# The causal mask added by VectorE instead of by an identity product, with new waits, in a hybrid decoder layer

## The chip, the cores and the metric

The program runs on one core of a Trainium2 chip. A core has five engines with queues of their own, each strictly in order: TensorE (PE; its weight loads are shown apart as PEld), VectorE (DVE), ScalarE (ACT), GpSimd (POOL) and SyncE (SP), which here only starts transfers. PE writes its results into PSUM, eight banks of 128 x 512 float32 numbers; DVE and ACT read and write both PSUM and the large on-chip memory, SBUF. The metric is the time of one execution on the device in microseconds (us).

## What is computed

One decoder layer on 256 tokens of width 1024: a combined projection whose columns are split into block-sparse attention (MoBA, 8 heads of 64) and retention (4 heads), an output projection, cross attention, and a gated feed-forward net, each with its norms and its residual. With 256 tokens there is a single key block, so that the attention is plain causal attention:

```python
proj = h @ w_in[l]
mq, mk, mv, rq, rk, rv, rg = jnp.split(proj, SPLIT_POINTS, axis=-1)
...
s_own = jnp.einsum('bhqd,bhld->bhql', qb, k_own).astype(jnp.float32) * scale
own_pos = cur * L + key_offsets
s_own = jnp.where(own_pos[None, :] <= q_pos[:, None], s_own, NEG_INF)
...
p = jax.nn.softmax(logits, axis=-1)
...
mix = jnp.concatenate([mo, ro], axis=-1) @ w_out[l]
x = x + rms_norm(mix, g_post_mix[l])
```

The change concerns the line with `jnp.where`: the scores of keys that lie after the query are made so small that their exponential is zero.

## The kernel before

Tokens lie in two tiles of 128 (t = 0 and 1). Weights come in blocks of 128 x 1024 float32 numbers, one transfer each, into a ring of six raw buffers (`rawp`, line 76); the block number q is in the names `raw13` and `hl13`. Each block is **split** (`split_weight`, lines 196 and 197): ACT copies it into a rounded form, DVE subtracts that from the original, and both parts together are `hl<q>`, in a ring of nine. A product with a block takes three passes of PE, high by high, high by low and low by high (lines 1114 to 1116), each 128 x 512.

The program is a list of **steps**, one for each piece of weight product, and PE executes them in that order. The side work (evictions, rotations, softmax, norms) is written as generators: each does a piece, yields a number from the table `WAIT` (line 38), and goes on that many steps later (`run_side`, line 259). So `WAIT` decides behind which weight product a piece stands, on every engine, and in which order the pieces stand on ACT and DVE. A weight block is split at the end of a step in which no side work ran, or when it is nearly due (line 1185 on). [...]

The first stage is the input projection in six chunks of columns: chunk 0 gives the queries, 1 the keys, 2 the retention's queries and keys (`ret_qk`), 3 its values, 4 its gate, 5 the attention's values. Each chunk has an accumulator for each token tile, named `acc<step>`: acc17 and acc18 are chunk 2, acc25 and acc26 chunk 3, acc33 and acc34 chunk 4. From chunk 2 on they come from a pool of **three** banks (`psB`, line 84). Chunk 3's are evicted by ACT into `rvd` (line 241). Transposes (c_q, c_k, c_r, c_R_mem, c_ro) all use **one** bank (`psC`, line 85), which ACT evicts. Softmax uses four banks (`psS`, line 83).

The attention is done in three units: m00 (queries of tile 0, all eight heads, 128 keys), m10 and m11 (queries of tile 1, four heads each, 256 keys). A unit goes in this order (`softmax_unit`, line 291; `moba_unit`, line 334): PE computes the scores into two banks `s_m`, and adds the mask there with a product of an identity matrix and the mask (lines 345 and 356: ahead of the scores in m11, behind them in the others); DVE takes the maxima (302) and their negative `nb` (306); ACT the exponentials (312); DVE normalizes (315, 317); PE transposes (`pt_m`, 325). Inside m11, right after its scores, the retention's scores `rs` are started.

Other names: `x_load` (line 1027) loads x and the constants on SP's queue; `x_stats` (1033) casts identity and mask for the products and has ACT take the mean squares of x (`junk`, 224); `mem_stats` (1011) does so for the memory rows. `xt_mix` and `xt_cross` (515) are the transposes of x behind the output projection and the cross attention; `xn` (509) is x scaled for the latter.

Of the kernel before, what the change touches and what calls it, by code (L numbers as in the profile page):

```python
# [8 lines left out]
F32R = mybir.dt.float32r  # L9
BF16 = mybir.dt.bfloat16  # L10
AF = mybir.ActivationFunctionType
ALU = mybir.AluOpType
AX = mybir.AxisListType

P = 128
# [21 lines left out]

WAIT = {
    "cpb0": 2, "cpb1": 1, "cpv0": 7, "cpv1": 1, "cu0": 3, "cu1": 4, "ex_c0": 2, "ex_c1": 1, "ex_m00": 0,
    "ex_m10": 0, "ex_m11": 4, "f0_0": 8, "f0_1": 5, "g_add": 1, "g_silu": 5, "gate0": 3, "gate1": 6,  # L40
    "gp1": 5, "gp2": 0, "k_add": 0, "k_hl": 3, "lag": 2, "ret": 9, "low": 6, "mq": 0, "mrow": 4, "ms": 21, "mst": 5,
# [5 lines left out]
}  # L47
WARM = 9

# [2 lines left out]
C_ID, C_MASK, C_MCOS, C_MSIN, C_RCOS, C_RSIN, C_DEC, C_END = 0, 128, 256, 288, 320, 448, 576, 1600  # L52
# [3 lines left out]
def tile_hybrid_layer(  # L56
# [14 lines left out]
    nc = tc.nc  # L71
    ctx.enter_context(tc.manual_schedule())

    cpool = ctx.enter_context(tc.tile_pool(name="cpool", bufs=1))
# [12 lines left out]
    def tok(t):  # L87
        return slice(t * P, (t + 1) * P)
# [4 lines left out]
    def small(name):  # L93
        return sm.tile([P, 8], F32, tag="sm", name=name)
# [10 lines left out]
    cst = cpool.tile([P, C_DEC], F32, tag="cst", name="cst")  # L105
    xg = cpool.tile([P, 288], F32, tag="xg", name="xg")
    gp = xg[:, 0:32].rearrange("p (g k) -> p g k", g=4)
    x_sb = cpool.tile([P, 2, D], F32, tag="x", name="x_sb")
    identb = cpool.tile([P, P], BF16, tag="identb", name="identb")
    maskb = cpool.tile([P, P], BF16, tag="maskb", name="maskb")  # L110
    identr = cpool.tile([P, P], F32R, tag="identr", name="identr")
    maskr = cpool.tile([P, P], F32R, tag="maskr", name="maskr")
    junk = cpool.tile([P, D], BF16, tag="junk", name="junk")
    mhalf = cpool.tile([P, 8], F32, tag="mhalf", name="mhalf")
    ident = cst[:, C_ID:C_ID + P]
# [5 lines left out]
    T = {}  # L121
# [3 lines left out]
    def need(*keys):  # L125

        missing = [k for k in keys if k not in emitted]
        assert not missing, missing
# [83 lines left out]
    def inv_rms(key, ss0, ss1=None, n=1):  # L212
        v = small(f"v_{key}")
        if ss1 is None:
            nc.vector.tensor_scalar(v[:, :n], ss0, EPS, None, op0=ALU.add)
        else:
            nc.vector.tensor_scalar(v[:, :n], ss0, ss1, EPS, op0=ALU.add, op1=ALU.add)
        r = cpool.tile([P, 8], F32, tag=f"r_{key}", name=f"r_{key}")
        nc.gpsimd.tensor_tensor(out=r[:, :n], in0=v[:, :n], in1=mhalf[:, :n], op=ALU.pow)
        rstd[key] = r  # L220
        return r

    def mean_square(dst, src, n):
        nc.scalar.activation(junk[:, :n], src, AF.Square, scale=1.0 / 32.0, accum_out=dst)
# [31 lines left out]
    def spawn(gen, wait=0):  # L256
        active.append([step_no[0] + wait, gen])
# [76 lines left out]
    def moba_unit(t, g):  # L334
        keys = P * (t + 1)
        n = D // keys
        hn = n // 2

        def fill(s):

            need(f"q{t}", *[f"k{u}" for u in range(t + 1)])

            ahead = g == 1
            for e in range(2) if ahead else ():
                nc.tensor.matmul(s[e].rearrange("p (h k) -> p h k", h=hn)[:, :, keys - P:keys], identr,
                                 maskr[:, None, :].to_broadcast([P, hn, P]), start=True, stop=False,
                                 skip_group_check=True)
            for i in range(hn):
                j = g * hn + i
                for e in range(2):  # L350
                    rows = slice(64 * e, 64 * e + 64)
                    nc.tensor.matmul(s[e][:, i * keys:(i + 1) * keys], T["qT"][rows, j, tok(t)],
                                     T["kT"][rows, j, 0:keys], start=(i == 0 and not ahead),
                                     stop=(ahead and i == hn - 1), skip_group_check=True)
            for e in range(2) if not ahead else ():
                nc.tensor.matmul(s[e].rearrange("p (h k) -> p h k", h=hn)[:, :, keys - P:keys], identb,
                                 maskb[:, None, :].to_broadcast([P, hn, P]), start=False, stop=True,
                                 skip_group_check=True)
            if ahead:
                scores = ret_scores()  # L360
                spawn(scores, next(scores))
            yield 0

        return softmax_unit(f"m{t}{g}", n, keys, 0.125, fill)

    def moba_units():
# [47 lines left out]
    def ret_scores():  # L414

        need("rqk0", "rqk1")
        for kb in range(2):
            n = P * (2 - kb)
            s = [accS(f"rs{kb}{e}") for e in range(2)]
            for j in range(2):  # L420
                for e in range(2):
                    rows = slice(64 * e, 64 * e + 64)
                    nc.tensor.matmul(s[e][:, j * n:(j + 1) * n], T["rkT"][rows, j, tok(kb)],
                                     T["rqT"][rows, j, kb * P:256], start=True, stop=True)
            for e in range(2):
                if kb == 0 or e == 0:
                    buf = tmp2k(f"ra{kb}{e}")
                a = buf[:, kb * e * 256:kb * e * 256 + 2 * n].rearrange("p (j i) -> p j i", j=2)
                T[f"ra{kb}{e}"] = a
                nc.vector.tensor_tensor(out=a, in0=s[e][:, 0:2 * n].rearrange("p (j i) -> p j i", j=2),  # L430
                                        in1=T["decay"].rearrange("p (j e) i -> p e j i", e=2)[:, e, :, 0:n], op=ALU.mult)
            if kb == 0:
                yield WAIT["rs"]
# [478 lines left out]
    for what in USE:  # L912
# [4 lines left out]
        elif what[0] == "d":  # L917
            k = int(what[1:])
# [17 lines left out]
    for q, item in enumerate(items):  # L936
        if item[0] == "w":
            continue
        kind, w, g, home, part, plus = item[:6]
# [91 lines left out]
        yield 0  # L1031

    def x_stats():
        nc.vector.tensor_copy(identb, ident)
        nc.vector.tensor_copy(maskb, cst[:, C_MASK:C_MASK + P])
        nc.vector.tensor_copy(identr, ident)
        nc.vector.tensor_copy(maskr, cst[:, C_MASK:C_MASK + P])
        for t in range(2):
            ss = small(f"ss_x{t}")
            mean_square(ss[:, 0:1], x_sb[:, t, :], D)  # L1040
            inv_rms(f"x{t}", ss[:, 0:1])
        yield 0
# [25 lines left out]
    x_split(2, 3)  # L1068
    opening = {4: lambda: x_split(4, 5), 7: lambda: x_split(6, 7)}
    late = {WAIT["xd"]: x_load, WAIT["xs"]: x_stats, WAIT["ms"]: mem_stats}  # L1070
    pending_split = list(range(2, NQ))

    accs, downs = {}, {}
    for i, s in enumerate(steps):
# [17 lines left out]
        if s[0] == "first":  # L1092
# [3 lines left out]
            h = hls[q][:, :, c * 512:(c + 1) * 512]  # L1096
# [6 lines left out]
        elif s[0] == "col":  # L1103
# [4 lines left out]
            h = hls[q].rearrange("p s (k n) -> p s k n", k=2)  # L1108
            for kk in range(2):
                k = 2 * kp + kk  # L1110
# [9 lines left out]
        elif s[0] == "row":  # L1120
# [13 lines left out]
            for k, w in ops:  # L1134
                begin = half == 0 and (k, w) == ops[0]
                end = half == 1 and (k, w) == ops[-1]
                if w:
                    nc.tensor.matmul(acc, hls[q][:, 0, k * P:(k + 1) * P], T[f"{st}_k"][:, k, :], start=begin, stop=end,  # L1138
                                     skip_group_check=True)
                else:  # L1140
                    nc.tensor.matmul(acc[:, 0:256], hls[q][:, 1, k * P:(k + 1) * P], T[st][:, 0, k, :], start=begin,  # L1141
                                     stop=end, skip_group_check=True)
            if half == 1:
                spawn(done(nt, acc))
        elif s[0] == "down":
            _, q, t, j, kk, halves = s
# [17 lines left out]
        elif s[0] == "seven":  # L1164
            _, q, g, m, part, name, begin = s
# [3 lines left out]
            h = hls[q].rearrange("p s (k n) -> p s k n", k=2)  # L1169
            for kk in range(2):  # L1170
                xh, xl = token_operand(m, 2 * part + kk)
                end = part == 1 and kk == 1
                for n, (a, w) in enumerate(((xh, 0), (xh, 1), (xl, 0))):
                    nc.tensor.matmul(acc, a, h[:, w, kk, :], start=begin and kk == 0 and n == 0, stop=end and n == 2,  # L1174
                                     skip_group_check=True)
# [9 lines left out]
        if pending_split:  # L1185
# [3 lines left out]
            hold = 0 <= i - starts["ffn"] + WAIT["hold0"] < WAIT["hold"] and q - s[1] > WAIT["hold_low"]  # L1189
            if q >= FFN_Q + 8:  # L1190
                paced = q not in after or split_at[after[q]] + WAIT["sum"] <= i
                near = due[q] - i <= (WAIT["near"] if i - split_at[q - 1] >= 2 else WAIT["now"])
            else:
                near = q - s[1] <= WAIT["low"]
# [113 lines left out]
```

## Time and profile before

| what | value |
|---|---|
| time, median of 3 runs | 398.38 us (398.0 to 398.8) |
| the profiled execution: its time | 400.7 us |
| its span, first to last instruction | 398.9 us |
| mean granted TensorE clock | 0.998 |
| DMA | 80.36 MB, mean 201 GB/s |

The granted clock of PE is at 90% or more in each of 40 slices of the span. DVE and ACT by slice (40 equal slices of 10 us, busy share in tenths):

```profile
DVE  3876877586869987677576699999899899999964
ACT  4885973964757865494547766766748685656741
```

The softmax units lie in the fourth to eighth slice, where both have room on the average. In rows of the timeline the columns are: start, duration, engine, line and operation, what is written and read with shapes, the count, and in brackets how long the engine stood idle before it and for what. Rows of one engine overlap a little at their ends, because an instruction's way out of the pipeline is counted with it.

### The profile page before, as it was taken

To read this page: it belongs to the slowest core of one execution; us is meant where nothing else is said; L and a number is where in the kernel's file an instruction comes from. 1 tells how busy PE (TensorE), PEld (TensorE's weight loads), DVE (VectorE), ACT (ScalarE), POOL (GpSimd) and SP (SyncE) were. 2 spreads that over 40 slices of the span, in tenths; PEclk is the share of its full clock that TensorE was granted. 3 is DMA by queue.
4 is the path that set the end of the run, shared out by engine and by line. 5 is a ranking of instruction groups with operands and counts; after the bars stand their busy time and mean duration, and the time that the engine had idled before them with its cause. 6 is when DMAs were issued, how large, how long until landed. Compare 5 with 4: busy or idle time off the path is not lost.

```text
span 398.9 us, 5470 instructions
## 1 busy us (share of the span) xinstructions
PE 390.0 (98%) x1969; PEld 323.9 (81%) x1969; DVE 320.3 (80%) x447; ACT 257.6 (65%) x431; POOL 33.4 (8%) x53
## 2 busy tenths in 40 slices
PE   7999999999999999999999999999999999999993
PEld 3888887888888888888888888888887888888882
DVE  3876877586869987677576699999899899999964
ACT  4885973964757865494547766766748685656741
POOL 0010020200011000000001001013113103101000
PEclk9999999999999999999999999999999999999999
DMA  8998837367547676607271459778939878954102
GB/s 275 414 354 268 300 118 252 107 187 287 168 152 223 200 215 204 214 4 235 79 263 55 158 193 358 242 157 315 278 72 279 241 242 175 372 191 71 38 0 105
DMA packets 23067, 80.36 MB, mean 201 GB/s; under 512 B 2560, under 2 KB 3200, under 8 KB 23040
## 3 DMA queue, kind: packets, MB, share of 16 engines
q1 hardware_dynamic: 18288, 62.97, 45.7%
q0 software_dynamic: 4608, 16.78, 17.1%
q8 instruction: 15, 0.25, 0.3%
q10 hardware_dynamic: 144, 0.26, 0.2%
q14 instruction: 12, 0.10, 0.1%
HBM read 78.95 MB, written 1.05 MB: 201 GB/s over the span
## 4 chain that ended last, share of the span: by engine, by line
PE 78%; issue 7%; DMA 7%; DVE 4%; ACT 1%; POOL 1%; SPq 0%; DVEq 0%; ACTq 0%; POOLq 0%
PE acc L1114 11%; PE acc L1116 11%; PE acc L1115 11%; PE acc L1138 7%; PE x L1174 7%; PE acc L1141 4%; PE down L1161 3%; PE down L1159 3%; PE down L1160 3%; PE y L1174 3%; DMA sum_qv<-in_weights_dram 3%; DVE hl L197 2%; PE acc L1102 2%; DMA sum_ret<-in_weights_dram 2%; DMA xr<-in_gx_dram 2%
## 5 line engine op out<-in xcount | busy, mean ns | idle before, releaser
L197 DVE TENSOR_TENSOR hl<-raw,hl 128x1024 fp32r<-128x1024 f32 (+1 forms) x102 | 119.3, 1189 | 16.9 <-ACT hl L196 16.8
L196 ACT ACTIVATE hl<-raw 128x1024 fp32r<-128x1024 f32 (+1 forms) x102 | 102.5, 1031 | 1.1 <-DMA raw<-in_weights_dram 0.9
L196 ACT ACTIVATE hl<-sum_qv 128x1024 fp32r<-128x1024 f32 x22 | 23.0, 1057 | 16.5 <-DVE sum_qv L203 12.9
L1114 PE MATMUL acc<-hl,xT 128*128 128x512 f32 x80 | 32.9, 411 | 0.0
L1159 PE MATMUL down<-hl,fT 128*128 128x512 f32 x80 | 31.3, 392 | 0.0
L1116 PE MATMUL acc<-hl,xT 128*128 128x512 f32 x80 | 31.3, 391 | 0.0
L1115 PE MATMUL acc<-hl,xT 128*128 128x512 f32 x80 | 31.2, 391 | 0.0
L1161 PE MATMUL down<-hl,fT 128*128 128x512 f32 x80 | 31.2, 390 | 0.0
L1160 PE MATMUL down<-hl,fT 128*128 128x512 f32 x80 | 31.1, 389 | 0.0
L197 DVE TENSOR_TENSOR hl<-sum_kT,hl 128x1024 fp32r<-128x1024 f32 x24 | 29.1, 1221 | 1.4 <-ACT hl L196 1.2
L196 ACT ACTIVATE hl<-sum_kT 128x1024 fp32r<-128x1024 f32 x24 | 24.8, 1051 | 5.5 <-DVE sum_kT L203 3.5
L197 DVE TENSOR_TENSOR hl<-sum_qv,hl 128x1024 fp32r<-128x1024 f32 x22 | 26.7, 1219 | 1.9 <-ACT hl L196 1.9
L1174 PE MATMUL x<-hl,comb 128*128 128x512 f32 x96 | 23.6, 392 | 0.4 <-DVE hl L197 0.4
L1174 PE MATMUL x<-hl,x2T 128*128 128x512 f32 x96 | 23.1, 392 | 0.0
L1174 PE MATMUL y<-hl,comb 128*128 128x512 f32 x96 | 23.1, 389 | 0.0
L1174 PEld LDWEIGHTS x<-hl,comb 128*128 128x128 f32 x96 | 17.9, 188 | 4.8 <-DVE hl L197 1.1
L1174 PEld LDWEIGHTS y<-hl,comb 128*128 128x128 f32 x96 | 18.0, 188 | 3.8
L1174 PEld LDWEIGHTS x<-hl,x2T 128*128 128x128 f32 x96 | 17.8, 188 | 3.6
L1161 PEld LDWEIGHTS down<-hl,fT 128*128 128x128 f32 x80 | 15.0, 188 | 3.3 <-DVE fT L664 0.2
L1116 PEld LDWEIGHTS acc<-hl,xT 128*128 128x128 f32 x80 | 15.0, 188 | 3.3
L1114 PEld LDWEIGHTS acc<-hl,xT 128*128 128x128 f32 x80 | 15.0, 188 | 3.2 <-issue 0.3
L1160 PEld LDWEIGHTS down<-hl,fT 128*128 128x128 f32 x80 | 15.0, 188 | 3.1
(260 smaller groups left out, 861.8 us busy)
## 6 DMA issues: line engine op xcount, KB each, us to landing
raw<-in_weights_dram SPq DMA_DIRECT2D x98, 512.0 KB, 4.8
sum_kT<-in_weights_dram POOLq DMA_DIRECT2D x14, 512.0 KB, 6.9
sum_qv<-in_weights_dram POOLq DMA_DIRECT2D x10, 512.0 KB, 5.7
sum_ret<-in_weights_dram POOLq DMA_DIRECT2D x8, 512.0 KB, 4.8
gpost<-in_gpost_dram SPq DMA_DIRECT2D x3, 512.0 KB, 5.2
x_sb<-in_x_dram SPq DMA_DIRECT2D x2, 512.0 KB, 8.1
memn<-in_mem_dram SPq DMA_DIRECT2D x2, 512.0 KB, 8.0
mr<-in_memT_dram SPq DMA_DIRECT2D x2, 512.0 KB, 7.4
```

The lines of the kernel that those rows point to most:

```text
L196: nc.scalar.activation(h[:, 0, n], raw[:, n], AF.Copy)
L197: nc.vector.tensor_tensor(out=h[:, 1, n], in0=raw[:, n], in1=h[:, 0, n].bitcast(F32), op=ALU.subtract)
L1102: nc.tensor.matmul(accs[(c, t)], T["xT"][:, hx, q, tok(t)], h[:, hw, :], start=begin, stop=False)
L1114: nc.tensor.matmul(acc, xh, h[:, 0, kk, :], start=(first and kk == 0), stop=False)
L1115: nc.tensor.matmul(acc, xh, h[:, 1, kk, :], start=False, stop=False)
L1116: nc.tensor.matmul(acc, xl, h[:, 0, kk, :], start=False, stop=(last and kk == 1))
L1138: nc.tensor.matmul(acc, hls[q][:, 0, k * P:(k + 1) * P], T[f"{st}_k"][:, k, :], start=begin, stop=end, skip_group_check=True)
L1141: nc.tensor.matmul(acc[:, 0:256], hls[q][:, 1, k * P:(k + 1) * P], T[st][:, 0, k, :], start=begin, stop=end, skip_group_check=True)
L1159: nc.tensor.matmul(acc, fh, wh, start=first, stop=False, skip_group_check=True)
L1160: nc.tensor.matmul(acc, fh, wl, start=False, stop=False, skip_group_check=True)
L1161: nc.tensor.matmul(acc, fl, wh, start=False, stop=last, skip_group_check=True)
L1174: nc.tensor.matmul(acc, a, h[:, w, kk, :], start=begin and kk == 0 and n == 0, stop=end and n == 2, skip_group_check=True)
```

## The change

VectorE adds the mask from the constants to the two banks of scores of each unit, in place, after the scores. The six mask products, the two identity and two mask operands and the four casts that made them are gone. 25 entries of the table of waits are other numbers; of these the diff shows the lines with xd, xs, ms, mst, ex_m11, mq and u2.

```diff
-    "ex_m10": 0, "ex_m11": 4, "f0_0": 8, "f0_1": 5, "g_add": 1, "g_silu": 5, "gate0": 3, "gate1": 6,
-    "gp1": 5, "gp2": 0, "k_add": 0, "k_hl": 3, "lag": 2, "ret": 9, "low": 6, "mq": 0, "mrow": 4, "ms": 21, "mst": 5,
+    "ex_m10": 0, "ex_m11": 8, "f0_0": 8, "f0_1": 5, "g_add": 1, "g_silu": 5, "gate0": 5, "gate1": 7,
+    "gp1": 0, "gp2": 0, "k_add": 0, "k_hl": 2, "lag": 2, "ret": 9, "low": 5, "mq": 3, "mrow": 5, "ms": 17, "mst": 7,
...
-            ahead = g == 1
-            for e in range(2) if ahead else ():
-                nc.tensor.matmul(s[e].rearrange("p (h k) -> p h k", h=hn)[:, :, keys - P:keys], identr,
-                                 maskr[:, None, :].to_broadcast([P, hn, P]), start=True, stop=False,
-                                 skip_group_check=True)
             for i in range(hn):
                 j = g * hn + i
                 for e in range(2):
                     rows = slice(64 * e, 64 * e + 64)
                     nc.tensor.matmul(s[e][:, i * keys:(i + 1) * keys], T["qT"][rows, j, tok(t)],
-                                     T["kT"][rows, j, 0:keys], start=(i == 0 and not ahead),
-                                     stop=(ahead and i == hn - 1), skip_group_check=True)
-            for e in range(2) if not ahead else ():
-                nc.tensor.matmul(s[e].rearrange("p (h k) -> p h k", h=hn)[:, :, keys - P:keys], identb,
-                                 maskb[:, None, :].to_broadcast([P, hn, P]), start=False, stop=True,
-                                 skip_group_check=True)
-            if ahead:
+                                     T["kT"][rows, j, 0:keys], start=(i == 0), stop=(i == hn - 1), skip_group_check=True)
+            for e in range(2):
+                diag = s[e].rearrange("p (h k) -> p h k", h=hn)[:, :, keys - P:keys]
+                nc.vector.tensor_tensor(out=diag, in0=diag, in1=cst[:, None, C_MASK:C_MASK + P].to_broadcast([P, hn, P]),
+                                        op=ALU.add)
+            if g == 1:
                 scores = ret_scores()
                 spawn(scores, next(scores))
...
-        nc.vector.tensor_copy(identb, ident)
-        nc.vector.tensor_copy(maskb, cst[:, C_MASK:C_MASK + P])
-        nc.vector.tensor_copy(identr, ident)
-        nc.vector.tensor_copy(maskr, cst[:, C_MASK:C_MASK + P])
```

Further: xs 11 to 7, xd 3 to 0 (x is loaded and its statistics taken earlier), u2 2 to 1 (m11 one step earlier). The new table moves pieces at many places. Three are shown, with the program's full names (block and tile numbers, then a running number).

DVE around the first unit's maxima, before:

```order
L197 TENSOR_TENSOR hl12_388<-raw12_260,hl12_388 128x1024
L197 TENSOR_TENSOR hl13_405<-raw13_293,hl13_405 128x1024
L302 TENSOR_REDUCE mx_m00_428<-s_m000_416 128x4
L302 TENSOR_REDUCE mx_m00_428<-s_m001_417 128x4
L306 TENSOR_SCALAR nb_m00_429<-mx_m00_428 128x8
L315 RECIPROCAL rs_m00_431<-sum_m00_430 128x8
L317 TENSOR_TENSOR p_m00_432<-p_m00_432,rs_m00_431 128x1024
L197 TENSOR_TENSOR hl14_457<-raw14_317,hl14_457 128x1024
```

and in the changed kernel:

```order
L193 TENSOR_TENSOR hl12_399<-raw12_274,hl12_399 128x1024
L346 TENSOR_TENSOR s_m000_410<-s_m000_410,cst_93 128x512
L346 TENSOR_TENSOR s_m001_411<-s_m001_411,cst_93 128x512
L298 TENSOR_REDUCE mx_m00_422<-s_m000_410 128x4
L298 TENSOR_REDUCE mx_m00_422<-s_m001_411 128x4
L302 TENSOR_SCALAR nb_m00_423<-mx_m00_422 128x8
L311 RECIPROCAL rs_m00_425<-sum_m00_424 128x8
L313 TENSOR_TENSOR p_m00_426<-p_m00_426,rs_m00_425 128x1024
L193 TENSOR_TENSOR hl13_446<-raw13_291,hl13_446 128x1024
```

The two additions stand between the split and the maxima, and the splits stand one block behind: hl13's is now after the unit's normalization.

ACT from the first unit's exponentials to the eviction of c_k1 into kr, before:

```order
L312 ACTIVATE p_m00_432,sum_m00_430<-s_m001_417,nb_m00_429 128x128 x4
L196 ACTIVATE hl14_457<-raw14_317 128x1024
L288 ACTIVATE qv_116<-c_q1_468 128x4x128
L241 ACTIVATE nat_r0_482<-acc17_368,r_x0_282 128x512
L196 ACTIVATE hl15_489<-raw15_335 128x1024
L241 ACTIVATE nat_r1_500<-acc18_375,r_x1_288 128x512
L330 ACTIVATE ptT_m00_514<-pt_m000_515 128x512
L196 ACTIVATE hl16_527<-raw16_366 128x1024
L288 ACTIVATE kr_117<-c_k1_539 128x4x128
```

and in the changed kernel:

```order
L308 ACTIVATE p_m00_426,sum_m00_424<-s_m001_411,nb_m00_423 128x128 x4
L192 ACTIVATE hl13_446<-raw13_291 128x1024
L284 ACTIVATE qv_112<-c_q1_457 128x4x128
L237 ACTIVATE nat_r0_469<-acc17_348,r_x0_240 128x512
L192 ACTIVATE hl14_476<-raw14_302 128x1024
L220 ACTIVATE junk_96,ss_mem0_487<-memn0_362 128x1024
L220 ACTIVATE junk_96,ss_mem1_493<-memn1_364 128x1024
L237 ACTIVATE nat_r1_499<-acc18_372,r_x1_246 128x512
L284 ACTIVATE kr_113<-c_k1_513 128x4x128
```

Both mean squares of the memory rows have come ahead of the eviction; the eviction of the transposed probabilities (ptT_m00) and one split have gone behind it.

ACT in the cross stage, from the mean square of x to the scaled x of tile 0 and what follows, before:

```order
L224 ACTIVATE junk_100,ssx_cross0_2073<-x_sb_95 128x1024
L196 ACTIVATE hl68_2099<-raw68_2001 128x1024
L509 ACTIVATE xn0_2110<-x_sb_95,r_x20_2077 128x1024
L196 ACTIVATE hl69_2118<-raw69_2013 128x1024
L224 ACTIVATE junk_100,ss_cross1_2129<-acc121_2079 128x512
```

and in the changed kernel:

```order
L220 ACTIVATE junk_96,ssx_cross0_2060<-x_sb_95 128x1024
L192 ACTIVATE hl67_2073<-raw67_1988 128x1024
L192 ACTIVATE hl68_2091<-raw68_2000 128x1024
L498 ACTIVATE xn0_2102<-x_sb_95,r_x20_2064 128x1024
L192 ACTIVATE hl69_2110<-raw69_2011 128x1024
```

The split of hl67, which had been done earlier, stands ahead of xn0; from hl69 on the order is that of before.

More of the change, by code (lines that the diff above doesn't have):

```diff
@@ L108, in tile_hybrid_layer @@
     x_sb = cpool.tile([P, 2, D], F32, tag="x", name="x_sb")
[L109 to L112, printed above, removed]
     junk = cpool.tile([P, D], BF16, tag="junk", name="junk")
```

10 rows, old and new, of the table WAIT are left out of this document.

## The prediction

> **What bounds the kernel now.** First the page: the engines' busy shares, then the chain that ended last.
>
> ```profile
> span 398.9 us, 5470 instructions
> ...
> PE 390.0 (98%) x1969; PEld 323.9 (81%) x1969; DVE 320.3 (80%) x447; ACT 257.6 (65%) x431; POOL 33.4 (8%) x53
> ...
> PE 78%; issue 7%; DMA 7%; DVE 4%; ACT 1%; POOL 1%; SPq 0%; DVEq 0%; ACTq 0%; POOLq 0%
> ```
>
> TensorE (PE) is busy nearly from end to end. So a product taken off PE shortens the span by what it takes, unless PE then arrives early at something that is not ready; and any wait put on PE lengthens the span by its whole size, since nothing later on PE is idle enough to take it back. The question is therefore not how much VectorE (DVE) has to do (80%), but whether the longer way of the softmax through DVE and ScalarE (ACT) is still done when PE asks for it. For that I read the timeline of the three engines from 30 to 70 us, row by row, and laid the new order of each engine over it.
>
> **What PE is spared.** Three softmax units (m00, m10, m11), two mask products each. The timeline of PE around each:
>
> ```profile
> 34.62 0.40 PE L1116 MATMUL acc<-hl,xT 128*128 128x512 f32 x1
> 34.95 1.16 PE L352 MATMUL s_m<-kr,qv 64*128 64x128 f32 x16
> 36.04 0.60 PE L356 MATMUL s_m<-maskb,identb 128*128 128x512 bf16 x2
> ...
> 36.71 0.40 PE L1115 MATMUL acc<-hl,xT 128*128 128x512 f32 x1
> ...
> 50.87 0.39 PE L356 MATMUL s_m<-maskb,identb 128*128 128x256 bf16 x2
> ...
> 51.33 0.40 PE L1115 MATMUL acc<-hl,xT 128*128 128x512 f32 x1
> ...
> 63.40 0.40 PE L1116 MATMUL acc<-hl,xT 128*128 128x512 f32 x1
> ...
> 63.96 1.14 PE L352 MATMUL s_m<-kr,qv 64*128 64x256 f32 x8
> ...
> 65.89 0.50 PE L1114 MATMUL acc<-hl,xT 128*128 128x512 f32 x1
> 66.22 0.40 PE L1115 MATMUL acc<-hl,xT 128*128 128x512 f32 x1
> ```
>
> Rows overlap at their ends, so I count from start to start. Where scores are followed directly by a weight product (65.89), the next one starts 0.33 later. Without its mask, m00's first weight product starts at 36.04 and the second at 36.37 instead of 36.71: 0.34. m10: 50.87 + 0.33 = 51.20 instead of 51.33: 0.13. m11, whose mask stands ahead of the scores: scores follow a weight product by 0.33 (34.62 to 34.95), so 63.73 instead of 63.96: 0.23. Together 0.70 us. The four casts that built the mask operands on DVE go too; nothing on PE waited for them, so 0.
>
> The new waits also put transposes side by side. A weight product after a transpose costs a little more than one after its like:
>
> ```profile
> 213.49 0.48 PE L1114 MATMUL acc<-hl,oT 128*128 128x512 f32 x1
> 213.80 0.40 PE L1115 MATMUL acc<-hl,oT 128*128 128x512 f32 x1
> 214.04 0.40 PE L1116 MATMUL acc<-hl,oT 128*128 128x512 f32 x1
> ```
>
> 0.31 against 0.24, some 0.08 for each change of kind. c_k1 now stands beside pt_m00 (one change fewer), and three of the four xt_mix groups stand together (two fewer): 0.24. What PE has to do thus shrinks by 0.94 us.
>
> **What DVE gets, and where.** The timeline of DVE from m00's maxima to those of m10:
>
> ```profile
> 36.47 1.29 DVE L302 TENSOR_REDUCE mx_m<-s_m 128x4 f32<-128x512 f32 x2
> 37.79 0.17 DVE L306 TENSOR_SCALAR nb_m<-mx_m 128x8 f32<-128x8 f32 x1
> 40.99 0.20 DVE L315 RECIPROCAL rs_m<-sum_m 128x8 f32<-128x8 f32 x1 [3.03 <-ACT p_m L312]
> ...
> 43.51 0.42 DVE L400 TENSOR_TENSOR rt_r<-nat_r,cst 128x256 f32<-128x256 f32 x1
> 43.84 0.42 DVE L402 TENSOR_TENSOR rt_r<-nat_r,cst 128x256 f32<-128x256 f32 x1
> 44.30 0.69 DVE L404 TENSOR_TENSOR nat_r<-nat_r,cst 128x512 f32<-128x512 f32 x1
> 45.02 0.69 DVE L405 TENSOR_TENSOR nat_r<-nat_r,rt_r 128x512 f32<-128x512 f32 x1
> ...
> 48.89 0.69 DVE L332 COPY ptT_m<-pt_m 128x512 f32<-128x512 f32 x1
> 49.49 1.22 DVE L197 TENSOR_TENSOR hl<-raw,hl 128x1024 fp32r<-128x1024 f32 x1
> ...
> 53.27 0.17 DVE L306 TENSOR_SCALAR nb_m<-mx_m 128x4 f32<-128x4 f32 x1
> ```
>
> Two things are to be seen. A pass over 128x512 out of a PSUM bank holds DVE for 0.60 (48.89 to 49.49), one over 128x256 for 0.33 (43.51 to 43.84). And from 40.99 to 53.27 no row has idle time: DVE is the engine that this stage goes by, from m00's exponentials to m10's. No row of this trace has DVE writing into a bank, so the price of an addition in place is bounded: from below by 0.33 for either width, from above by the 0.72 of two operations where one needs the other (44.30 to 45.02). I take 0.60 and 0.33, from the rows of their widths: m00 2 x 0.60 = 1.20, m10 2 x 0.33 = 0.66, together **1.86 us** (1.3 to 2.9).
>
> The Trainium skill (VectorE: DVE Perf Modes, section "The perf-mode tier table") speaks against a cheap addition: an fp32 tensor_tensor with an operand in PSUM has no mode faster than one element a cycle. By that page's 0.96 GHz an estimate would be at least 0.53 and 0.27 an addition, 1.6 us together, and the sum below would end 0.26 lower. The rows of 0.60 and 0.33 agree with it, and by that rule my lower end is too low.
>
> The additions wait for the scores, which PE ends by 36.1, so DVE does not stand for them; behind them in DVE's queue stand the maxima, the normalization and every later split. Nothing ahead takes the 1.86 off: m00's maxima start at 36.47 because the subtraction ahead of them ends there, which the new order keeps (hl12 in the place of hl13). Between the units DVE has the same list as before in both orders (two rotations, one copy, three subtractions, two statistics), so m10's exponentials start 1.86 later.
>
> **Where it meets PE.** ACT, and the product that waits for it:
>
> ```profile
> 53.53 0.48 ACT L312 ACTIVATE p_m<-s_m,nb_m 128x256 f32<-128x256 f32 x1 [2.55 <-DVE nb_m L306]
> ...
> 57.51 1.28 ACT L241 ACTIVATE rvd<-acc,r_x 128x512 f32<-128x512 f32 x2
> ```
>
> ```profile
> 58.50 0.48 PE L1114 MATMUL acc<-hl,xT 128*128 128x512 f32 x1
> ```
>
> ACT waits 2.55 us for DVE there, then does exponentials, a split, R_mem, another split and the two evictions of chunk 3's accumulators. That list is unchanged and takes 57.51 - 53.53 = 3.98. The product at 58.50 begins chunk 4's second accumulator; there are three such banks, so it needs the first of those two, free at 57.51 + 0.64 (half of 1.28) = 58.15. Now: 53.53 + 1.86 + 3.98 + 0.64 = 60.01, and with 0.05 for the signal **60.06: PE stands 1.56 later there than before, whatever it saved up to then**. Behind this product stands all the rest of PE's work, in order.
>
> An earlier wait is swallowed by this one. The eviction of c_k1 frees the only transpose bank for c_r0:
>
> ```profile
> 44.41 0.60 ACT L330 ACTIVATE ptT_m<-pt_m 128x512 f32<-128x512 f32 x1
> 44.91 1.05 ACT L196 ACTIVATE hl<-raw 128x1024 fp32r<-128x1024 f32 x1
> 46.68 0.60 ACT L288 ACTIVATE kr<-c_k 128x512 f32<-128x512 f32 x1 [0.72 <-PE c_k L287]
> 47.17 1.05 ACT L224 ACTIVATE junk<-memn 128x1024 bf16<-128x1024 f32 x1
> ...
> 49.40 1.05 ACT L196 ACTIVATE hl<-raw 128x1024 fp32r<-128x1024 f32 x1
> ```
>
> ```profile
> 47.88 0.60 PE L409 MATMUL c_r<-cst,nat_r 128*128 128x128 f32 x4
> ```
>
> It could have run at 46.68 - 0.72 = 45.96. Now ptT_m00 (0.50) and a split (1.05) come behind it, both mean squares (49.40 - 47.17 = 2.23) ahead, and m00's exponentials are 1.20 late: 45.96 - 1.55 + 2.23 + 1.20 = 47.84, done at 48.44. PE would be at c_r0 a little before 47.88, so it waits some 0.7.
>
> After 58.50: m11's mask is spared (0.23); its additions stand on DVE while PE computes the retention scores, and ACT is idle there, so 0 (0.66, two of 0.33, if that cover were gone). Two changes of kind fewer at xt_mix: 0.16. In the cross stage a split now stands ahead of xn0:
>
> ```profile
> 210.28 1.04 ACT L196 ACTIVATE hl<-raw 128x1024 fp32r<-128x1024 f32 x1
> 211.22 1.15 ACT L509 ACTIVATE xn<-x_sb,r_x 128x1024 f32<-128x1024 f32 x1
> ...
> 213.13 0.60 PE L515 MATMUL xt_cross<-cst,xn 128*128 128x128 f32 x4
> ```
>
> xn0 is ready at 212.37 and needed at 213.13; 0.94 later (210.28 to 211.22) it is ready at 213.31, with the signal 0.23 late. x, its statistics' source, is loaded ahead of two weights instead of behind them on SP's queue:
>
> ```profile
> 21.04 1.06 ACT L224 ACTIVATE junk<-x_sb 128x1024 bf16<-128x1024 f32 x1 [1.27 <-DMA x_sb<-in_x_dram]
> ...
> 22.35 1.06 ACT L224 ACTIVATE junk<-x_sb 128x1024 bf16<-128x1024 f32 x1 [0.16 <-DMA x_sb<-in_x_dram]
> ```
>
> Such transfers land 1.31 apart, so x lands some 2.6 earlier and hl6's split moves behind both statistics. I take 0, since the wait at 58.50 swallows it; alone it could cost up to one landing, 1.3. The post gains' load, moved forward past three weights on SP, waits for DVE's last read of its buffer; the six raw buffers ahead cover it, and if they did not, it would cost a landing too.
>
> **Sum.** 1.56 - 0.23 - 0.16 + 0.23 = +1.40. The profiled execution has a span of 398.9 and lasted 400.7; it would be 400.3 and 402.1. It stands 2.3 above the median of 398.38, to which I add the same 1.40: **399.8 us**. With the additions at their bounds, 399.2 to 400.8.
>
> **Rivals.** (1) **Faster**: the chain from the additions to chunk 3's eviction has room that I do not see (an accumulator that takes another bank, or work that leaves DVE's list), and PE keeps its 0.94: 397.4. For it: 3.03 and 2.55 us idle stand on DVE and ACT in that stage. Against: both idle times are waits within this very chain. It decides for itself at 58.50: if the eviction is late by under 0.35 (58.15 to 58.50), nothing is lost. (2) **No change**: the additions take about 0.35 each, some 1.3 together, and xn0 is not late: 1.3 - 0.35 + 0.05 - 0.39 = 0.6 at most, 398.4 to 399.1. (3) **Worse**: additions in a bank at 0.72 and more, and the early load of x or m11's additions stop PE besides: 400.8 and above.
>
> **How the numbers follow.** Forecast 0.58, rival (1) 0.16, (2) 0.18, (3) 0.08. A range of 398.0 to 400.8 holds the forecast, (2) and the edge of (3). By 0.2% (0.8 us, about what a measurement of this kernel can tell from none): faster 0.15, same 0.21, slower 0.64.
>
> **What would show it.** m00's DVE rows: two additions from 36.5, 0.60 apart, exponentials at 39.25. PE idle ahead of c_r0 (0.7, ACT kr), ahead of chunk 4's second accumulator (about 1.1, ACT rvd), ahead of xt_cross (0.2, ACT xn); PE's own work 0.9 shorter. If PE has no idle row between 40 and 62 us, the forecast is wrong, and the time falls.

## The result, and the profile after

| kernel | median | ratio to before (95% interval) |
|---|---|---|
| before | 398.38 us (398.0 to 398.8, 6 runs) | |
| changed | 400.42 us (400.0 to 400.88, 6 runs) | 1.0051 (1.0038 to 1.0064) |

The changed kernel is slower by 2.04 us, by the interval of the ratio by 1.5 to 2.5. The forecast was +1.4, 399.8 us.

The profile of the changed kernel, its page first:

```profile
span 398.3 us, 5458 instructions
...
PE 389.8 (98%) x1963; PEld 323.6 (81%) x1963; DVE 322.5 (81%) x449; ACT 257.5 (65%) x431; POOL 33.2 (8%) x53
...
PE 90%; DVE 5%; ACT 3%; issue 1%; POOL 0%; DVEq 0%; ACTq 0%
```

The span is shorter than the 398.9 of before, though the kernel is slower. The profiled execution of before was one of its long ones (400.7 us against a median of 398.38), so the kernel before was profiled once more. Its page then:

```profile
span 396.4 us, 5470 instructions
...
PE 389.3 (98%) x1969; PEld 324.4 (82%) x1969; DVE 320.3 (81%) x447; ACT 258.0 (65%) x431; POOL 33.3 (8%) x53
...
PE 98%; DVE 0%; ACT 0%; DVEq 0%; issue 0%; ACTq 0%
```

This execution took 398.16 us, and its span is 1.9 below that of the changed kernel, as the medians have it. All comparisons below are with this second profile. What is to be read in the chains: before, the work that ended last is a chain of PE alone (98%). After, 5% of the span stands on DVE and 3% on ACT, though the share of DVE's busy time is the same 81%: some 30 us of work on these two engines have come onto the path, most of it between 33 and 59 us.

The summary of PE's waits says where the path comes back to PE. The columns are who waited, for whom, the sum, how often, and the longest. Of before (second profile) and of after:

```profile
PE warm L980 <- PEq L1298: 0.8, 1, 0.8
```

```profile
PE acc L1099 <- ACT rvd L237: 0.8, 1, 0.8
PE warm L969 <- PEq L1283: 0.8, 1, 0.8
PE c_r L398 <- ACT kr L284: 0.5, 1, 0.5
```

The warm-up is in both. New are the two waits that the prediction named: c_r0 for ACT's eviction `kr`, and chunk 4's second accumulator for ACT's eviction `rvd`. The third that it named, 0.2 at xt_cross, is too short for this list and stands in the table of the section on why. The DVE rows in between, after:

```profile
35.25 1.29 DVE L346 TENSOR_TENSOR s_m<-s_m,cst 128x512 f32<-128x512 f32 x2
36.45 1.28 DVE L298 TENSOR_REDUCE mx_m<-s_m 128x4 f32<-128x512 f32 x2
...
51.84 0.76 DVE L346 TENSOR_TENSOR s_m<-s_m,cst 128x256 f32<-128x256 f32 x2
52.51 1.28 DVE L298 TENSOR_REDUCE mx_m<-s_m 128x2 f32<-128x512 f32 x2
```

and the same maxima before (second profile):

```profile
34.80 1.29 DVE L302 TENSOR_REDUCE mx_m<-s_m 128x4 f32<-128x512 f32 x2
...
50.21 1.28 DVE L302 TENSOR_REDUCE mx_m<-s_m 128x2 f32<-128x512 f32 x2
```

From start to start the pair of m00 takes 36.45 - 35.25 = 1.20, that of m10 52.51 - 51.84 = 0.67: 1.87 us against 1.86 forecast. But m10's maxima are 52.51 - 50.21 = 2.30 later, because DVE's part also begins 35.25 - 34.80 = 0.45 later than it did. And where the chain meets PE, after:

```profile
46.29 0.39 PE L1101 MATMUL acc<-hl,xT 128*128 128x512 f32 x1
47.22 0.66 PE L398 MATMUL c_r<-cst,nat_r 128*128 128x128 f32 x4 [0.54 <-ACT kr L284]
...
57.45 0.60 PE L398 MATMUL c_r<-cst,nat_r 128*128 128x128 f32 x4
58.88 0.50 PE L1099 MATMUL acc<-hl,xT 128*128 128x512 f32 x1 [0.82 <-ACT rvd L237]
```

and before:

```profile
56.29 0.39 PE L1116 MATMUL acc<-hl,xT 128*128 128x512 f32 x1
56.52 0.60 PE L409 MATMUL c_r<-cst,nat_r 128*128 128x128 f32 x4
56.88 0.48 PE L1114 MATMUL acc<-hl,xT 128*128 128x512 f32 x1
```

A transpose follows a weight product by 0.23 (56.29 to 56.52), and four transposes are followed by a product after 0.36. So c_r0 stood for 0.93 - 0.23 = 0.70 and chunk 4's second accumulator for 1.43 - 0.36 = 1.07. The brackets (0.54 and 0.82) are smaller, since part of a gap is counted as the end of the product ahead of it; starts are the better measure. Chunk 4's second accumulator begins 58.88 - 56.88 = 2.00 later, and behind it little of that is taken back.

### The profile page after: what moved, and what is told of

Same layout as the page of the kernel before. It is cut to its first block, busy times and chain, and to the rows that moved or that the text cites. A ratio compares the mean times of both kernels' runs of the same rounds, so it can differ in the third digit from the quotient of the medians.

```text
span 398.3 us, 5458 instructions
## 1 busy us (share of the span) xinstructions
PE 389.8 (98%) x1963; PEld 323.6 (81%) x1963; DVE 322.5 (81%) x449; ACT 257.5 (65%) x431; POOL 33.2 (8%) x53
## 4 chain that ended last, share of the span: by engine, by line
PE 90%; DVE 5%; ACT 3%; issue 1%; POOL 0%; DVEq 0%; ACTq 0%
PE x L1159 11%; PE acc L1099 10%; PE acc L1100 10%; PE acc L1101 10%; PE acc L1123 9%; PE y L1159 5%; PE down L1146 5%; PE down L1144 5%; PE down L1145 5%; PE acc L1126 5%; PE acc L1087 3%; PE z L1159 3%; DVE hl L193 1%; ACT hl L192 1%; ACT p_m L308 1%
```

## The experiments

Theory: m00's and m10's additions lie in a stretch of DVE without idle time, whose end (through m10's exponentials and chunk 3's evictions) decides when PE can begin chunk 4's second accumulator. Rival: the additions are hidden and the new numbers of waits cost the time. Medians are beside runs of the kernel before on the same chip, 398.38 to 398.51 us.

### The kernel before, once more

> The kernel before, profiled once more. Its first profiled execution took 400.7 us, 2.3 above its median of 398.38, and has two waits of PE that the profile of the changed kernel has not: 1.31 at the start (the gap ahead of the first product of weights is 1.79 us against 0.48) and 0.44 at 304.5. If these belong to that one execution, this one has a gap of about 0.5 at the start, takes 398.4 to 399.4 and has a span of 396.6 to 397.6, so that the spans of before and after differ by +0.7 to +1.7 as the medians (+2.04) have it. If they belong to the kernel, this one shows both again at about 400.7, and the change itself took 1.75 away at places that the prediction had not priced.

398.16 us, span 396.4, both 0.2 below the lower ends that were expected. Neither wait is there: the two belonged to that one execution. Nothing in the prediction's sum rested on them, but the two spans by themselves would have given the change a gain of 0.6 us.

### The two halves of the change apart

The first kernel has the additions with the old numbers of waits, the second the products on PE with the new ones. The edit of each is one half of the diff above. The third is the changed kernel with the mask left out:

```diff
-            for e in range(2):
-                diag = s[e].rearrange("p (h k) -> p h k", h=hn)[:, :, keys - P:keys]
-                nc.vector.tensor_tensor(out=diag, in0=diag, in1=cst[:, None, C_MASK:C_MASK + P].to_broadcast([P, hn, P]),
-                                        op=ALU.add)
```

> The changed kernel with the numbers of waits of the kernel before: only the mask's additions stand against the kernel before. Theory (the additions in VectorE's chain set the end): the exponentials of m10 are 1.86 us later, the second accumulator of chunk 4 begins 1.56 later whatever PE saved ahead of it, and m11 gives 0.23 back behind it: 398.38 + 1.3 = 399.7 us, with PE idle some 1.5 at that product, and nothing new at c_r0, at the first use of the sixth split and at xt_cross. Rival (the new waits are to blame): PE's 0.70 and 0.09 come through, 397.6 us. By the first, the new waits cost about 0.7 of the 2.04; by the second, all of it and more.

> The kernel before, mask products on PE and all, with the new numbers of waits. Theory: without the additions the exponentials of m10 end early enough that chunk 4's second accumulator does not wait; what the waits cost by themselves is 0.25 at the first use of the sixth split and 0.13 at c_q (x loaded early), 0.22 at xt_cross (xn0 behind a split), against 0.16 of fewer changes of kind: 398.38 + 0.4 = 398.8 us. Rival (the new waits are to blame): PE still stands at c_r0 for 0.6 and at chunk 4's second accumulator for 0.8, and the time is 400.2 us or more.

> The changed kernel without the additions: the mask is left out of the scores, nothing else differs. Theory, counted from the kernel before by the prediction's terms: 398.38 less 0.94 on PE, plus 0.38 of the early load of x, plus 0.22 at xt_cross = 398.0 us. Counted from the changed kernel by the two waits that its trace lays to the chain (0.59 at c_r0, 0.83 at chunk 4's second accumulator): 400.42 less 1.42 = 399.0. The two do not agree by 1.0 us; the run says which sum lacks a term. Rival (the additions are hidden, the new waits cost the time): 400.2 us or more.

| kernel | median | ratio to before |
|---|---|---|
| additions, old waits | 399.85 us | 1.0035 (1.0023 to 1.0047) |
| products, new waits | 398.80 us | 1.0007 (0.9998 to 1.0017) |
| no mask, new waits | 398.28 us | 0.9994 (0.9985 to 1.0002) |

The theory holds in all three: 399.7, 398.8 and 398.0 to 399.0 were expected, and the rival's 397.6, 400.2 and 400.2 are far off. The additions alone cost 399.85 - 398.39 = 1.46 us, the new waits with them another 400.42 - 399.85 = 0.57, the new waits without them 398.80 - 398.39 = 0.41, at the edge of what can be told from none. Of the two sums for the kernel without a mask, 398.0 came nearer than 399.0: the second had sized the two waits by brackets (0.59 and 0.83), not by starts (0.70 and 1.07).

The first of the three also settles whether the wait at c_r0 is swallowed by the later one. It has the old order on ACT and no wait at c_r0 at all. Its rows on DVE and PE:

```profile
35.08 1.29 DVE L346 TENSOR_TENSOR s_m<-s_m,cst 128x512 f32<-128x512 f32 x2
```

```profile
57.20 0.66 PE L398 MATMUL c_r<-cst,nat_r 128*128 128x128 f32 x4
58.72 0.50 PE L1099 MATMUL acc<-hl,xT 128*128 128x512 f32 x1 [0.87 <-ACT rvd L237]
```

Additions begin 0.17 earlier than in the changed kernel (35.08 against 35.25), and the product 0.16 earlier (58.72 against 58.88). With or without 0.70 lost at c_r0, the product begins by DVE's chain, 23.6 us behind the additions. PE's wait there is 58.72 - 57.20 - 0.36 = 1.16 and not the 1.5 expected; another 0.19 stands ahead of the transposes c_r1 at 57.20 (0.42 behind the product before them, where 0.23 is usual), and the end is the same.

### More additions; the eviction moved; m11 alone; the load of x

Each addition once more:

```diff
+            for e in range(2):
+                diag = s[e].rearrange("p (h k) -> p h k", h=hn)[:, :, keys - P:keys]
+                nc.vector.tensor_tensor(out=diag, in0=diag, in1=cst[:, None, C_MASK:C_MASK + P].to_broadcast([P, hn, P]),
+                                        op=ALU.add)
```

> The changed kernel with each of the six additions and once more (the second adds the same mask again, which changes no probability that is not already zero). Theory: m00's and m10's second additions lie in VectorE's unbroken chain too, so the exponentials of m10 are another 1.86 us later (2 x 0.60 + 2 x 0.33), PE stands at chunk 4's second accumulator for 2.7 in place of 0.8, and the time is 400.42 + 1.86 = 402.3 us; m11's second additions cost nothing. Rival (additions are hidden behind PE and the waits cost the time): 400.4 to 400.8 us.

402.33 us, ratio 1.0101 (1.0087 to 1.0116): 1.91 more than the changed kernel, as expected. The trace shows it where the theory has it, on DVE 36.45 to 37.64 for the second pair of m00, and in the summary of PE's waits (the warm-up left out):

```profile
PE c_k L283 <- ACT qv L284: 1.1, 1, 1.1
PE acc L1103 <- ACT rvd L237: 0.9, 1, 0.9
...
PE c_r L402 <- ACT kr L284: 0.5, 1, 0.5
PE c_r L402 <- ACT R_mem L245: 0.4, 1, 0.4
```

By starts, PE's waits at c_r0 (0.66) and at chunk 4's second accumulator (1.16) are about what they are in the changed kernel (0.70 and 1.07). New are 1.28 at the transposes c_k1 and 0.55 at c_r1. The expectation put the whole 2.7 at one product. It came in pieces, two of them at transposes that had not waited for the one bank, but with the same end: chunk 4's second accumulator begins at 60.76, 1.88 later than in the changed kernel.

The additions kept, the two evictions of chunk 3 issued ahead of the weight splits:

```diff
+        if key == "m10":
+            emitted.add("ex_m10")
...
+            if "ex_m10" in emitted and "rv1" not in emitted:
+                hold = True
```

> The changed kernel, additions and all, with weight splits held back from m10's exponentials until the two evictions of chunk 3 are issued: on ScalarE these stand behind the eviction of R_mem, with two splits ahead of them no longer. Theory: PE's wait of 0.83 at chunk 4's second accumulator (three banks, the first accumulator of chunk 3 not yet evicted) goes, the wait of 0.59 at c_r0 stays: 400.42 - 0.8 = 399.6 us. Rival one: the splits held back are late in their turn and PE waits for them in the same stage: 400.2 us or more. Rival two: the product waits for something else than the bank (its weights), and the wait stays as it is: 400.4 us.

398.99 us, ratio 1.0018 (1.0009 to 1.0027): 1.43 better than the changed kernel, more than the 0.8 expected, which again went by the bracket; by starts the wait was 1.07. ACT and PE of this kernel:

```profile
55.83 0.39 ACT L245 ACTIVATE R_mem<-c_R_mem 128x256 f32<-128x256 f32 x1
56.09 1.29 ACT L237 ACTIVATE rvd<-acc,r_x 128x512 f32<-128x512 f32 x2
57.23 1.09 ACT L192 ACTIVATE hl<-raw 128x1024 fp32r<-128x1024 f32 x1
```

```profile
57.31 0.60 PE L400 MATMUL c_r<-cst,nat_r 128*128 128x128 f32 x4
57.67 0.48 PE L1101 MATMUL acc<-hl,xT 128*128 128x512 f32 x1
```

Product follows transposes by 0.36: the wait is gone. So it was the bank, and what held the bank was not the exponentials alone but also two splits that ACT did ahead of the evictions in the changed kernel, 0.95 us each. From the changed kernel the product comes 58.88 - 57.67 = 1.21 forward. The edit does more than it was made for: the wait of 0.22 at xt_cross is gone too (212.04 to 212.26 from product to transposes, 0.22 where 0.45 stood), and `ro` now waits 0.20 (0.43 behind its product, where 0.23 is usual). The span is 1.1 shorter, 397.2 us; the rest of the 1.43 between medians is not found in the trace.

From the kernel before, m11's mask alone goes to DVE, with the waits at xt_mix of the changed kernel:

```diff
-            ahead = g == 1
-            for e in range(2) if ahead else ():
-                nc.tensor.matmul(s[e].rearrange("p (h k) -> p h k", h=hn)[:, :, keys - P:keys], identr,
...
+            plain = g == 1
...
+                if plain:
+                    nc.vector.tensor_tensor(out=diag, in0=diag, in1=cst[:, None, C_MASK:C_MASK + P].to_broadcast([P, hn, P]),
+                                            op=ALU.add)
+                else:
+                    nc.tensor.matmul(diag, identb, maskb[:, None, :].to_broadcast([P, hn, P]), start=False, stop=True,
+                                     skip_group_check=True)
```

> The kernel before with m11's mask alone added by VectorE (m00's and m10's stay products on PE), and of the new numbers only the five waits at xt_mix. Theory: m11's additions fall where VectorE waits for others and PE for none of it, so PE's 0.23 comes through, and 0.16 of the changes of kind at xt_mix: 398.38 - 0.4 = 398.0 us, at the edge of what can be told from no change. Rival: the additions of m11 delay the evictions that follow them on VectorE, 398.7 us or more.

397.73 us, ratio 0.9991 (0.9981 to 1.0). Its times lie in two groups, six from 397.6 to 397.7 us and four from 398.3 to 398.5, so the median alone says little. No rows of it are shown; the same kernel stands again further on, with a profile.

The load of x at its old place, in the changed kernel:

```diff
-"xd": 0
+"xd": 3
...
-"xs": 7
+"xs": 11
```

> The changed kernel with the two waits of the load of x as before, so that x and the constants come behind two more blocks of weights. By the prediction (all that is lost ahead of chunk 4's second accumulator is swallowed by the wait there): the waits of 0.25 at the sixth split and 0.13 at c_q go, the wait at chunk 4's second accumulator grows by as much, 400.4 us. Rival: the lag begins before m00's scores, where VectorE's chain itself begins, and moves the whole chain: 400.42 - 0.4 = 400.0 us.

399.81 us, ratio 1.0041 (1.0026 to 1.0055). The median is 0.61 below that of the changed kernel; the two intervals overlap, so the trace has to say it. PE at the sixth split and at m00's scores, changed kernel first:

```profile
21.47 0.39 PE L1099 MATMUL acc<-hl,xT 128*128 128x512 f32 x1
21.84 0.50 PE L1100 MATMUL acc<-hl,xT 128*128 128x512 f32 x1
...
33.82 1.16 PE L342 MATMUL s_m<-kr,qv 64*128 64x128 f32 x16
```

```profile
21.40 0.39 PE L1099 MATMUL acc<-hl,xT 128*128 128x512 f32 x1
21.63 0.39 PE L1100 MATMUL acc<-hl,xT 128*128 128x512 f32 x1
...
33.46 1.16 PE L342 MATMUL s_m<-kr,qv 64*128 64x128 f32 x16
```

The lead grows from 0.07 to 0.36 between, so the early load costs PE 0.29 ahead of m00's scores. Of the two waits that were expected to go, the 0.25 at the sixth split went; the one of 0.13 at c_q stayed (0.36 from product to transposes in both kernels, 0.23 before), so another of the new waits makes it; which one is not shown. And this kernel keeps its wait for the bank as it was, 0.8 in the summary of PE's waits, with 0.5 at c_r0:

```profile
34.89 1.29 DVE L346 TENSOR_TENSOR s_m<-s_m,cst 128x512 f32<-128x512 f32 x2
```

The additions begin 0.36 earlier (34.89 against 35.25), and chunk 4's second accumulator 0.34 (58.54 against 58.88). So the rival was right in the main: what PE loses this early is not swallowed, because it moves the chain that the wait belongs to. Where that chain leaves PE is seen in the chain that ended last of the changed kernel (start, us, what, with the overlap of rows taken off):

```profile
32.06 0.45 PE c_k L283 x4
...
33.02 1.06 ACT hl L192
34.11 1.22 DVE hl L193
35.33 1.21 DVE s_m L346 x2
...
58.25 0.58 ACT rvd L237
58.88 0.50 PE acc L1099
```

It is not m00's scores, as the rival had it, but the transposes c_k0 ahead of them: ACT evicts these (`kr`), then copies a block for its split, DVE subtracts for that split, and the additions follow without idle time.

### The memory's statistics, all repairs together, m11 again

The two waits of the memory's statistics as before, in the changed kernel:

```diff
-"ms": 17
+"ms": 21
...
-"mst": 7
+"mst": 5
```

> The changed kernel with the two waits of the memory's statistics as before (the memory's load two weights later, its two mean squares behind the eviction of c_k1 on ScalarE); with that order the eviction of chunk 3's first accumulator also moves ahead of R_mem. Prediction: PE's wait of 0.59 at c_r0 goes, but the wait at chunk 4's second accumulator grows by what is saved, less the 0.26 by which the eviction moves ahead: 400.42 - 0.26 = 400.2 us, with a wait of 1.1 there in place of 0.8. Rival: the two waits add up, and 0.6 comes through: 399.8 us or less, with the wait there unchanged.

401.32 us, ratio 1.0069 (1.0054 to 1.0083): slower, which neither side expected; most of that is a second loss, behind the stall and not in every execution, which the last section tells. The wait at c_r0 went, but the new order on ACT put R_mem behind both splits and one `rvd`, and c_R_mem holds the one transpose bank that c_r1 needs. PE of this kernel:

```profile
56.37 0.39 PE L1101 MATMUL acc<-hl,xT 128*128 128x512 f32 x1
58.76 0.66 PE L398 MATMUL c_r<-cst,nat_r 128*128 128x128 f32 x4 [2.01 <-ACT R_mem L245]
59.18 0.48 PE L1099 MATMUL acc<-hl,xT 128*128 128x512 f32 x1
```

One wait of 2.39 - 0.23 = 2.16 stands where two stood. The edit thus changed more than it was to change, and does not separate the two theories; the kernel with old waits above does.

Then the edits of three kernels together, those of the held splits, of the load of x and of the memory's statistics:

> The changed kernel, all three masks added by VectorE, with the three repairs together: the splits held back until chunk 3's evictions, the two waits of the load of x and the two of the memory's statistics as before. Theory: where the bank's wait is out of the way, c_r0's 0.6 and the 0.36 by which e7's chain began earlier come through in full: 398.99 - 0.96 = 398.0 us, and the additions' 1.86 in VectorE's chain then cost nothing that PE sees. Rival: a next wait of the same chain (m10's transposes, or the eviction of chunk 3's second accumulator) takes their place: 398.7 us or more.

398.54 us, ratio 1.0001 (0.9993 to 1.001): level with the kernel before, with all three masks on DVE. The additions' 1.87 in DVE's chain is there as before, but PE waits for it no longer where it did. 0.5 of the expected gain did not come: 0.28 stands ahead of c_r1, since R_mem, now between the two `rvd`, frees the transpose bank late (0.51 from start to start on PE, 56.67 to 57.18, where 0.23 is usual), a small wait of the same chain, as the rival had it. `ro` begins 0.59 behind its product, 0.16 more than with the held splits alone. The summary puts that to ACT's exponentials of m11, and in this kernel's chain that ended last m11's additions (63.05 on DVE) stand ahead of them, so they are not free here. The rest, some 0.1, is not found.

And the kernel with m11's mask alone on DVE, once more:

> The same kernel as e6_last_mask_added, for a profile and a second interval: e6's profiled execution took 1680 us with each matrix product four times as long as in every other, and shows nothing of the kernel. Theory: 397.7 to 398.0 us, PE's stretches to 110 us without a new wait, m11's additions on VectorE in time that it had idle. Rival: e6's median was the lower of two groups (397.7 and 398.4) by chance, and the time is 398.4 us.

398.04 us, ratio 0.9991 (0.9983 to 1.0). Twice the same ratio, which stands for 0.36 us, near the two terms (0.23 and 0.16), and both intervals end at 1.0: likely a small gain, smaller than can be told with certainty. The median lies between the theory's 398.0 and the rival's 398.4, nearer to the theory. DVE at m11 in this kernel:

```profile
61.82 1.21 DVE L195 TENSOR_TENSOR hl<-raw,hl 128x1024 fp32r<-128x1024 f32 x1
63.72 0.76 DVE L352 TENSOR_TENSOR s_m<-s_m,cst 128x256 f32<-128x256 f32 x2 [0.68 <-PE s_m L346]
```

Here DVE stood idle for 0.68 before the additions, waiting for PE's scores, and PE waits for nothing but its warm-up. The same addition that cost its full length in m00 and m10 is free in m11 of this kernel.

## Why the prediction was right or wrong

The direction and the main mechanism were right (additions in DVE's chain, paid at the bank that ACT frees), and the size was 0.6 short of the median, mainly because a term was put at nothing.

| term of the sum | forecast | shown |
|---|---|---|
| additions in DVE's chain | 1.86 | 1.87 (1.20 + 0.67, from start to start) |
| wait at c_r0, swallowed | 0.7 | 0.70, swallowed (old waits with additions) |
| wait at chunk 4's second accumulator | 1.1 | 1.07 |
| lateness of that product | 1.56 | 2.00 |
| m11's mask off PE | -0.23 | -0.23 (weight products 59.22 against 57.19 ahead, 72.27 against 70.47 behind) |
| changes of kind at xt_mix | -0.16 | -0.09 (100.21 against 98.42 ahead, 135.57 against 133.87 behind) |
| xn0 behind a split | +0.23 | +0.22 (212.96 against 211.28 ahead, xt_cross 213.41 against 211.51) |
| early load of x | 0 | +0.3 in the trace, 0.6 between medians |
| wait at c_q, ahead of m00's scores | not in the sum | +0.13 |

- **The additions** were priced from two rows that were no additions, a copy out of a bank and a rotation, and both prices held to 0.01 a pair. That DVE had no idle row there decided what they cost. The Trainium skill (VectorE: DVE Perf Modes, section "The perf-mode tier table") gives an fp32 tensor_tensor with an operand in PSUM no mode faster than one element a cycle; 0.60 and 0.33 an addition in the bank itself agree with that.
- **The step that failed** is "I take 0, since the wait at 58.50 swallows it", of the early load of x. A wait swallows only what is lost behind the point where its own chain leaves PE. That point is c_k0, the transposes ahead of m00's scores. c_r0 lies behind it and was swallowed; the load of x lies ahead of it, so it moved DVE's chain and with it the wait, by 0.29 in the trace. The wait of 0.13 at c_q, which the sum does not have at all, lies ahead of it too.
- **The lateness of that product**, 2.00, adds up from the rows. Additions 1.87; early load 0.29; c_q 0.13. Less 0.28 that the product had to spare before (1.04 us from the evictions' start at 55.84 to the product at 56.88, against 0.76 now, 58.12 to 58.88), and less 0.09 because m00's maxima began 1.23 behind the subtraction ahead of them before and the additions 1.14 now. That is 1.9; the last 0.1 is the start of the program, since the weight product at 21.47, ahead of all of this, is already 0.11 behind its like in the execution of before (21.36).
- **PE's savings** came as counted: from the scores to the second product behind them 1.43 us in place of 1.77 in m00 and 1.39 in place of 1.53 in m10, and 0.23 in m11. Those of m00 and m10 were swallowed, as forecast: without additions and without products, the new waits give 398.28, with products 398.80. So 0.52 of the 0.70 does come through once no chain stands in its way.
- **Changes of kind**: 0.16 was forecast at xt_mix and 0.09 is shown, with three groups of transposes side by side as the prediction had it. Why the second change gave nothing is not shown.
- **What remains**: the spans differ by 1.9; less 0.1 for the start that is 1.8 in the trace, against 2.04 (1.5 to 2.5) between medians. The rest is within the interval.
- **The rivals**: the unseen room of the first was not there as written, but a form of it was. Two splits ahead of the evictions can be moved, and that gave 1.4 back. Of the third, the early load of x did stop PE, but for 0.3 and not for a landing.

## What to carry to other kernels

Whether an operation may be moved to another engine is read from that engine's idle time at the very place, not from its share of the span: the same addition cost all its length in m00 and m10 and nothing in m11 of the changed kernel, with DVE at 81%. A wait swallows an earlier delay only if that delay lies behind the point where the waited-for chain leaves the waiting engine; follow the chain back to find it. When a chain gets longer, look at what else is queued ahead of its last step: two splits held back bought more than half of the loss.

## What the runs showed of the hardware

**Behind a stall of 2 us, PE's clock fell to half.** In the kernel with the memory's statistics moved, the windows of PE around the stall (from and to, width, PE busy, granted clock, DMA share, GB/s):

```profile
56.00:59.50 3.50, 1.49 (x10) 1.00 0.00 0
59.50:63.40 3.90, 3.90 (x16) 0.56 0.93 292
63.40:67.00 3.60, 3.60 (x24) 1.00 0.50 149
```

and its rows there:

```profile
59.96 0.63 PE L1099 MATMUL acc<-hl,xT 128*128 128x512 f32 x1
60.38 0.63 PE L1100 MATMUL acc<-hl,xT 128*128 128x512 f32 x1
```

Products are 0.42 apart in place of 0.23, for some 3.4 us (a mean of 0.56 over 3.90 us is 3.4 us at half). Three of its six executions took 401.8 to 402.0 us at a mean clock of 0.992 to 0.993, the other three 400.4 to 400.9 at 0.995 to 0.997, level with the changed kernel (400.0 to 400.9). One of the six has a profile; that the other two long ones had the same stretch, and that it cost the 1.4, is read from their mean clock. In the profile of the kernel with doubled additions, whose longest gap between starts from 40 to 70 us is 1.5 us, the clock there is 1.00 throughout. Heavy transfers alone do not do it: in the kernel with m11's mask alone on DVE the DMA share is 0.94 from 60 to 63 us, at a clock of 1.00. That the stall is the cause is likely from this, and not shown by a run that changes it alone. The Trainium skill (TensorE: Matmul & The Clock Gate, section "Part 1: The HAM clock gate (the "warmup" mystery)") has PE go to half its clock after an idle window of about 3.4 us, in windows that run free. The length of the slow stretch and its coming in only some executions agree with it. The idle time does not: here the longest gap between starts ahead of the stretch is 2.4 us.
